# Norms whose two-input work leaves GpSimd, and a first ConvFFN pair that takes one token stream at a time

## The chip, the cores and the metric

The kernel runs on one core of one Trainium2 chip. The metric is the device time of one execution in microseconds (us). The engines are called TensorE (PE in the profile, its weight load PEld), VectorE (DVE), ScalarE (ACT), GpSimd (POOL) and SyncE (SP, which issues most transfers).

## The reference

One inference step of a decoder trunk of two layers over 544 tokens: 512 of a new sequence and 8 x 4 sampled ones. The model dimension is 1024, that of the ConvFFN 2816.

```python
for i in range(2):
    h = rms_norm(x, norm_mix[i])
    x = x + (conformer_conv(h) if i == 0 else stick_breaking_attention(h))
    h = rms_norm(x, norm_ffn[i])
    g = h @ w_gate[i]
    x = x + (silu(causal_dwconv(g)) * (h @ w_up[i])) @ w_down[i]
y = rms_norm(x, norm_final)
```

`rms_norm(x, g)` is `x * rsqrt(mean(x*x) + eps) * g` for each token, over the 1024 channels. The depthwise convolution of the ConvFFN (`causal_dwconv`) has a width of three tokens, so that a channel's gate is needed for all tokens before its taps. The outputs also hold the new rows of the convolution states and of keys and values.

## The kernel before, in words

**Layout.** `x` lies transposed in SBUF as `xT`: 128 partitions x 8 chunks `c` x 544 tokens. The tokens form two streams, SA (columns 0 to 255) and SB (the other 288, the sampled ones among them). A product of 128 output channels with one stream is a group of 24 matmuls into one PSUM bank. Each factor is split into a high and a low part, and a chunk takes three matmuls: `whi` by `XH`, `whi` by `XL`, `wlo` by `XH` (`gemm`, L425 to L427; in the ConvFFN `part`, L1251 to L1253; later quads L1439 to L1441).

**Weights.** A ring holds them: SyncE loads a `raw` slot, ScalarE copies it to `whi` (L325), VectorE subtracts for `wlo` (L328). Five slots are split ahead; when a slot is freed, the next is prepared.

**A norm** (class `Norm`, L489). When a chunk of `xT` has been evacuated (VectorE adds the PSUM bank to `x`: L1149, in the ConvFFN of layer 0 L1598), `feed` squares it on ScalarE (L516) and adds the square to the running sum `sqa` (L521). The add of the last chunk runs on VectorE, those of chunks 1 to 6 on GpSimd. The steps that follow are: `rstd` (a matmul with the matrix `mean_m` at L532, the root on ScalarE at L534, the reciprocal on VectorE at L535); then for each chunk the scaled `u = xT * rstd` (L539, for chunks 1, 2, 3, 5, 6 and 7 on GpSimd, `POOL_U`, and otherwise on VectorE), `XH` from `u` on ScalarE (L542) and `XL` from `u` and `XH` on VectorE (L545).

**Two ways of ordering.** Around the products of the mixers and the last downs the order is written by hand. `feed` issues its instructions in place, and the steps go into a queue `side`, of which `some` takes one at each quarter of a product. `take_due` puts a finished norm's steps into it: in `run_group` (L440) at quarter `DUE[last]` of a stream's first product, in `Wide` (L457) at quarter 3. In the ConvFFN and around the convolution a planner (class `Plan`, L75) orders the work: each operation comes with an engine, a cost and what it reads and writes, and the planner lays the operations out by these costs, with `urgent` as a bonus. The planned version of SB's norm ahead of a ConvFFN is `norm()` (L1272: matmul L1277, reciprocal L1282, `u` L1286, `XH` L1288, `XL` L1290); those of the convolution phase have their adds at L1092 and their `u` at L1123. Each engine executes its instructions in the order that results, so one that waits holds all behind it.

**The ConvFFN.** The hidden channels are taken in passes. The first pass begins with two pairs of channel groups by `gate_plain` (L1404) and `up` (L1496), called at L1573: gate 0 and gate 1 for SA, then both for SB, evacuated by ScalarE into `G`, then the taps of the width-three convolution (`taps`, VectorE L1393 and others), and then up 0 for SA and SB and up 1 for SA and SB; VectorE multiplies with the silu of the taps (L1504), and `low_h` splits the result into `HH` (ScalarE) and `HL` (VectorE, L1493). These products use the banks `tr` and `av` by turns (`psum2`, two of each); the tag `acc` has four. Pairs behind the first pass are taken as quads. After a pass come the downs of its channels and the transposes of the state rows (L1554).

**The final norm** (`Final.feed`) squares (L1637), adds chunks 1 to 6 on GpSimd (L1645) and transposes; L1680 to L1688 scale the rows.

Of the kernel before, what the change touches and what calls it, by code (L numbers as in the profile page):

```python
# [14 lines left out]
ALU = mybir.AluOpType  # L15
# [180 lines left out]
def tile_trunk(  # L196
# [260 lines left out]
    class Wide:  # L457


        def __init__(self, xh, xl, evac):  # L460
            self.xh, self.xl, self.evac = xh, xl, evac
# [27 lines left out]
    class Norm:  # L489
# [21 lines left out]
        def feed(self, st, c):  # L511
            c0, n = st
            if st is SA and c == 4:
                act_table("sqrt_and_others")
            sq = self.tile("sq", 3) if c else self.tile("sqa", 2)
            act.activation(sq[:, :n], xT[:, c, c0:c0 + n], AF.Square)  # L516
            if c == 0:
                self.acc[st] = sq
            else:
                a = self.acc[st][:, :n]  # L520
                (dve if c == NC - 1 else pool).tensor_tensor(a, sq[:, :n], a, op=ALU.add)  # L521
            if c == NC - 1:
                due.append(self.steps(st))

        def steps(self, st):
            c0, n = st
            cols = slice(c0, c0 + n)
            hold = {}

            def rstd():  # L530
                pt = bank("tr", uid("ms"))
                pe.matmul(pt[:, :n], mean_m, self.acc[st][:, :n], start=True, stop=True)  # L532
                hold["r"] = self.tile("rstd", 2)
                act.activation(hold["r"][:, :n], pt[:, :n], AF.Sqrt, bias=eps_t[:, 0:1], scale=1.0)  # L534
                dve.reciprocal(hold["r"][:, :n], hold["r"][:, :n])  # L535

            def scaled(c):
                u = hold[c] = self.tile("u", NC)
                (pool if c in POOL_U else dve).tensor_tensor(u[:, :n], xT[:, c, cols], hold["r"][:, :n], op=ALU.mult)  # L539

            def high(c):
                act.activation(XH[:, c, cols], hold[c][:, :n], AF.Copy, scale=pcol(self.row, c))  # L542

            def low(c):
                dve.scalar_tensor_tensor(XL[:, c, cols], hold[c][:, :n], pcol(self.row, c), XH[:, c, cols],  # L545
                                         op0=ALU.mult, op1=ALU.subtract)
# [86 lines left out]

    def psum(tag):
        return plan.tile(tag, banks[tag], lambda: bank(tag, uid(tag)))

    def on(eng, n, dve_cost, pool_cost):
        return (dve, "dve", 0.08 + n * dve_cost) if eng == "dve" else (pool, "pool", 0.1 + n * pool_cost)

    def product(slot, h):  # L640

# [439 lines left out]
    def normed(c, h):  # L1081

        c0, n = STREAMS[h]
        sq = plan.tile("sq" if c else "sqa", 2, lambda: nrm.tile("sq" if c else "sqa", 2))
        plan.op("act", 0.1 + n * 0.9e-3, lambda: act.activation(sq()[:, :n], xT[:, c, c0:c0 + n], AF.Square),
                r=[("x", c, h), "norm"], w=[sq])
        if c == 0:
            nrm.acc[h] = sq
            return
        a = nrm.acc[h]  # L1090
        e, name, cost = on("dve" if c == NC - 1 else "pool", n, 1.05e-3, 2.25e-3)
        plan.op(name, cost, lambda: e.tensor_tensor(a()[:, :n], sq()[:, :n], a()[:, :n], op=ALU.add), r=[sq], w=[a])  # L1092

    s0 = slot_no[0]
    slot_no[0] += NC
# [23 lines left out]
    plan.op("dve", 1.7, lambda: dve.reciprocal(rs()[:, :n], rs()[:, :n]), w=[rs])  # L1119
    for c in range(NC):  # L1120
        u = plan.tile("u", NC, lambda: nrm.tile("u", NC))
        e, name, cost = on("pool" if c in POOL_U else "dve", n, 1.05e-3, 2.25e-3)
        plan.op(name, cost, lambda c=c, u=u, e=e: e.tensor_tensor(u()[:, :n], xT[:, c, 0:n], rs()[:, :n], op=ALU.mult),  # L1123
                r=[rs, ("x", c, 0)], w=[u])
        plan.op("act", 0.32, lambda c=c, u=u: act.activation(XH[:, c, 0:n], u()[:, :n], AF.Copy,
                                                             scale=pcol(R_FFN, c)), r=[u], w=[("XH", c, 0)])
# [31 lines left out]
    def ffn(l, before, after):  # L1158
# [95 lines left out]

            return plan.op("pe", len(xs) * 3 * n * 0.4615e-3, f, w=[pt], r=[("slot", slot), *rd], follows=name)

        def group(slot, st, nk, xh, xl, keys):

            c0, n = st
            pt = psum2()  # L1260
# [11 lines left out]
        def norm():  # L1272
# [2 lines left out]
            pt, rs = psum("tr"), plan.tile("rstd", 2, lambda: before.tile("rstd", 2))  # L1275
            plan.op("in", ACC_LATE, lambda: None, w=["acc"])
            plan.op("pe", 0.55, lambda: pe.matmul(pt()[:, :n], mean_m, before.acc[SB][:, :n], start=True, stop=True),  # L1277
                    r=["acc"], w=[pt], urgent=2.0)
            plan.op("act", 0.36, lambda: act.activation(rs()[:, :n], pt()[:, :n], AF.Sqrt, bias=eps_t[:, 0:1], scale=1.0),
                    r=[pt, "table"], w=[rs])  # L1280
            plan.op("act", 1.3, lambda: act_table("silu_and_others"), w=["table"])
            plan.op("dve", 1.9, lambda: dve.reciprocal(rs()[:, :n], rs()[:, :n]), w=[rs])  # L1282
            for c in range(NC):
                u = plan.tile("u", NC, lambda: before.tile("u", NC))
                e, name, cost = (pool, "pool", 0.9) if c in POOL_U else (dve, "dve", 0.43)
                plan.op(name, cost, lambda c=c, u=u, e=e: e.tensor_tensor(u()[:, :n], xT[:, c, cols], rs()[:, :n], op=ALU.mult),  # L1286
                        r=[rs], w=[u])
                plan.op("act", 0.45, lambda c=c, u=u: act.activation(XH[:, c, cols], u()[:, :n], AF.Copy,  # L1288
                                                                   scale=pcol(before.row, c)), r=[u], w=[("X", c, 1, "h")])
                plan.op("dve", 0.5, lambda c=c, u=u: dve.scalar_tensor_tensor(  # L1290
                    XL[:, c, cols], u()[:, :n], pcol(before.row, c), XH[:, c, cols], op0=ALU.mult, op1=ALU.subtract),
                    r=[u, ("X", c, 1, "h")], w=[("X", c, 1), "normed"])

# [107 lines left out]
            plan.op("pool", 0.2, lambda: pool.tensor_copy(  # L1401
                SF[:, f, 2:18].rearrange("p (b t) -> p b t", b=NB), gs()[:, :, 4:6]), r=[g], w=[("SF", f)])

        def gate_plain(f2, s0):  # L1404
            gs = [G(f2 + i) for i in range(2)]
            for st in (SA, SB):
                for i in range(2):
                    pt = group(s0 + i, st, NC, XH, XL, xkeys)
                    c0, n = st
                    m, dst, new = places(gs[i], c0, n)  # L1410
                    plan.op("act", acost(m), lambda dst=dst, pt=pt, m=m: act.copy(dst(), pt()[:, :m]), r=[pt], a=[gs[i]])
                    if n > m:
                        plan.op("act", 0.2, lambda new=new, pt=pt, m=m, n=n: act.copy(new(), smp(pt(), m, n)), r=[pt], a=[gs[i]])
            for i in range(2):
                used(s0 + i)
                taps(f2 + i)

        def products(slots, tags, put):

# [73 lines left out]
            plan.op("dve", dcost(T), lambda: dve.tensor_tensor(  # L1493
                HL[:, f - k0, :], h(), HH[:, f - k0, :], op=ALU.subtract), r=[h], w=[("H", f - k0)])

        def up(f2, slots, k0):  # L1496
            for i in range(2):
                f = f2 + i
                h = buf(None, "h", [P, T], H_BUFS)
                s = sil[f]  # L1500
                for st in (SA, SB):
                    c0, n = st
                    pt = group(slots[i], st, NC, XH, XL, xkeys)
                    plan.op("dve", dcost(n), lambda c0=c0, n=n, pt=pt, h=h, s=s: dve.tensor_tensor(  # L1504
                        h()[:, c0:c0 + n], s()[:, c0:c0 + n], pt()[:, :n], op=ALU.mult), r=[pt, s], a=[h], urgent=U_POST)
                used(slots[i])
                low_h(f, k0, h)

        def up_quad(f2, slots, k0):
            hs = [buf(None, "h", [P, T], H_BUFS) for _ in range(2)]  # L1510

# [58 lines left out]
        s = first  # L1570
        (k0, nk), *rest = PASSES
        for f2 in range(k0, k0 + nk, 2):
            gate_plain(f2, s)  # L1573
            up(f2, (s + 2, s + 3), k0)
            s += 4

        for p0, pn in rest:
# [32 lines left out]
    class Final:  # L1610
# [17 lines left out]
        def feed(self, st, c):  # L1628
# [13 lines left out]
                                 for _ in self.blocks(st)]  # L1642
            elif c < NC - 1:
                a = self.acc[st][0][:, :n]
                pool.tensor_tensor(a, sq[:, :n], a, op=ALU.add)  # L1645

            def turn():
                if c % 4 == 0:
# [685 lines left out]
```

## Time and profile before

| | |
|---|---|
| time, median of 3 runs | 1355.88 us (1354.37 to 1357.83) |
| the profiled execution | 1356.08 us |
| its span in the trace | 1354.4 us |
| TensorE clock granted, mean | 0.992 |
| moved by DMA | 142.39 MB, 105 GB/s |
| GpSimd adds of squares L521 | 24, 23.3 us |
| GpSimd scaled chunks L539, L1286 | 18 and 12, 17.7 and 11.5 us |
| GpSimd work in the convolution phase L1092, L1123 | 12 and 6, 13.0 and 5.1 us |
| GpSimd adds of the final norm L1645 | 12, 9.2 us |

How to read the rows of the profile: a group of instructions shows line, engine, operation, out<-in by the program's names with partitions x elements, count | busy us, mean ns of one | idle time of the engine ahead of them, and what ended it. A row of the timeline shows its start in us from the span's start, how long it took (several instructions together where xN says so) and, in brackets, the engine's idle time before it and what ended that. A row of the waits shows the instruction that waited, what it waited for, and then the us in total, the times and the longest. A row of the windows shows the stretch, its length, and the busy time and the instructions of each engine in it. Matmuls overlap: their spacing, not their duration, says what one costs.

### The profile page before, as it was taken

What the parts mean: (1) busy time and instruction counts of PE and PEld (TensorE: products, weight loads), DVE (VectorE), ACT (ScalarE), POOL (GpSimd) and SP (SyncE); (2) the same over time, 40 slices, a digit from 0 to 9 for tenths busy, and PEclk for the clock granted to TensorE, in tenths of its full rate; (3) what the DMA queues carried; (4) which work ended last, traced back from release to release, by engine and by line L of the source; (5) the groups of instructions that cost most, each with busy time, mean ns of one, the idle gap of its engine ahead of it and who ended that gap; (6) DMA issues with size and microseconds to landing.
All of it is one profiled execution on the core that took longest, in us unless ns stands there. A gap on an engine that the chain in (4) does not pass through costs nothing.

```text
span 1354.4 us, 26784 instructions
## 1 busy us (share of the span) xinstructions
PE 1318.0 (97%) x11018; PEld 1242.8 (92%) x11018; DVE 975.6 (72%) x1650; ACT 668.9 (49%) x1242; POOL 240.5 (18%) x379
## 2 busy tenths in 40 slices
PE   8999999999999999998999999999899999999997
PEld 7897799899999999998999777769899999999997
DVE  5599785878987877856253776663897896786762
ACT  6421574545554554544333566753654654454452
POOL 3201014301010010033221242222520010000012
PEclk9899999999999999999999999999999999999998
DMA  8273523123233233235365242322122233233221
GB/s 227 67 185 103 126 95 109 32 86 102 87 111 101 73 111 114 76 118 181 126 205 166 80 129 90 102 94 63 63 79 83 92 110 110 75 100 109 86 73 66
DMA packets 124492, 142.39 MB, mean 105 GB/s; under 512 B 5672, under 2 KB 117992, under 8 KB 124099
## 3 DMA queue, kind: packets, MB, share of 16 engines
q1 hardware_dynamic: 118003, 122.43, 29.4%
q0 software_dynamic: 6080, 18.25, 4.3%
q8 instruction: 86, 1.41, 0.4%
q14 instruction: 35, 0.29, 0.1%
q10 hardware_dynamic: 288, 0.02, 0.0%
HBM read 129.34 MB, written 12.18 MB: 104 GB/s over the span
## 4 chain that ended last, share of the span: by engine, by line
PE 84%; DVE 9%; ACT 3%; issue 1%; DMA 1%; POOL 0%; SPq 0%; DVEq 0%; ACTq 0%; POOLq 0%
PE acc L1441 5%; PE acc L1439 5%; PE acc L1440 5%; PE acc L425 4%; PE acc L426 4%; PE acc L427 4%; PE tr L1252 4%; PE tr L1251 4%; PE tr L1253 3%; PE av L1251 3%; PE av L1252 3%; PE av L1253 3%; PE acc L651 3%; PE acc L653 3%; PE acc L652 3%; PE tr L1441 3%
## 5 line engine op out<-in xcount | busy, mean ns | idle before, releaser
L328 DVE TENSOR_TENSOR wlo<-raw,whi 128x1024 fp32r<-128x1024 f32 (+2 forms) x244 | 258.5, 1064 | 77.5 <-ACT whi L325 77.1
L325 ACT CAST whi<-raw 128x1024 fp32r<-128x1024 f32 (+2 forms) x244 | 223.0, 916 | 153.5 <-PE tr L1252 30.5
L651 PE MATMUL acc<-XH,whi 128*128 128x288 f32 (+1 forms) x384 | 114.9, 299 | 0.0
L653 PE MATMUL acc<-XH,wlo 128*128 128x288 f32 (+1 forms) x384 | 111.0, 289 | 1.8 <-DVE wlo L328 1.8
L652 PE MATMUL acc<-XL,whi 128*128 128x288 f32 (+1 forms) x384 | 111.3, 290 | 0.0
L425 PE MATMUL acc<-XH,whi 128*128 128x288 f32 (+1 forms) x360 | 107.8, 300 | 0.6 <-DVE xT L1598 0.6
L426 PE MATMUL acc<-XL,whi 128*128 128x288 f32 (+1 forms) x360 | 104.0, 289 | 0.0
L427 PE MATMUL acc<-XH,wlo 128*128 128x288 f32 (+1 forms) x360 | 103.6, 288 | 0.0
L1441 PE MATMUL acc<-TH,wlo 128*128 128x272 f32 x288 | 83.4, 290 | 0.0
L1439 PE MATMUL acc<-TH,whi 128*128 128x272 f32 x288 | 83.2, 289 | 0.0
L1440 PE MATMUL acc<-TL,whi 128*128 128x272 f32 x288 | 83.1, 288 | 0.0
L1475 ACT COPY G<-acc 128x272 f32<-128x272 f32 (+1 forms) x72 | 26.9, 373 | 110.3 <-PE acc L1441 95.4
L651 PEld LDWEIGHTS acc<-XH,whi 128*128 128x128 f32 x384 | 72.7, 189 | 2.7 <-issue 2.1
L653 PEld LDWEIGHTS acc<-XH,wlo 128*128 128x128 f32 x384 | 72.8, 190 | 2.2 <-DVE wlo L328 2.2
L1252 PE MATMUL av<-HL,whi 128*128 128x288 f32 (+1 forms) x256 | 74.4, 290 | 0.0
L1251 PE MATMUL av<-HH,whi 128*128 128x288 f32 (+1 forms) x256 | 74.3, 290 | 0.0
L1253 PE MATMUL av<-HH,wlo 128*128 128x288 f32 (+1 forms) x256 | 74.0, 289 | 0.0
L1251 PE MATMUL tr<-HH,whi 128*128 128x256 f32 (+1 forms) x256 | 73.6, 288 | 0.0
L1252 PE MATMUL tr<-HL,whi 128*128 128x256 f32 (+1 forms) x256 | 73.4, 287 | 0.0
L652 PEld LDWEIGHTS acc<-XL,whi 128*128 128x128 f32 x384 | 72.8, 190 | 0.5
L1253 PE MATMUL tr<-HH,wlo 128*128 128x256 f32 (+1 forms) x256 | 73.0, 285 | 0.0
L1393 DVE SCALAR_TENSOR_TENSOR cv<-G,fprm,cv 128x560 f32<-128x560 f32 x88 | 69.9, 798 | 4.2 <-ACT cv L1390 3.0
(461 smaller groups left out, 4456.0 us busy)
## 6 DMA issues: line engine op xcount, KB each, us to landing
raw<-in_ffn_w_gate_dram SPq DMA_DIRECT2D x22, 1024.0 KB
raw<-in_ffn_w_up_dram SPq DMA_DIRECT2D x22, 1024.0 KB
raw<-in_ffn_w_down_dram SPq DMA_DIRECT2D x24, 768.0 KB
raw<-in_attn_w_qkv_dram SPq DMA_DIRECT2D x12, 1024.0 KB
raw<-in_conv_w_in_dram SPq DMA_DIRECT2D x6, 1024.0 KB
rep<-glu SPq DMA_DIRECT2D x36, 142.0 KB
raw<-in_conv_w_out_dram SPq DMA_DIRECT2D x4, 1024.0 KB
raw<-in_ffn_w_down_dram SPq DMA_DIRECT2D x8, 512.0 KB
```

What stands on the lines that cost most here:

```text
L325: act.copy(hi[:, :n, :], src)
L328: dve.tensor_tensor(lo[:, :n, :], src, hi[:, :n, :], op=ALU.subtract)
L425: pe.matmul(o, hi[:, k, :], xh[:, k, c0:c0 + n], start=(k == 0), stop=False)
L426: pe.matmul(o, hi[:, k, :], xl[:, k, c0:c0 + n], start=False, stop=False)
L427: pe.matmul(o, lo[:, k, :], xh[:, k, c0:c0 + n], start=False, stop=(k == nk - 1))
L651: pe.matmul(o, hi[:, k, :], XH[:, k, c0:c0 + n], start=(k == 0), stop=False)
L652: pe.matmul(o, hi[:, k, :], XL[:, k, c0:c0 + n], start=False, stop=False)
L653: pe.matmul(o, lo[:, k, :], XH[:, k, c0:c0 + n], start=False, stop=(k == NC - 1))
L1251: pe.matmul(o, hi[:, j + k, :], xh, start=(start and k == 0), stop=False, **kw)
L1252: pe.matmul(o, hi[:, j + k, :], xl, start=False, stop=False, **kw)
L1253: pe.matmul(o, lo[:, j + k, :], xh, start=False, stop=(stop and k == len(xs) - 1), **kw)
L1441: pe.matmul(o, lo[:, j + k, :], xh, start=False, stop=(k == 3), **kw)
```

## The change

Four things are edited. (1) Every add of squares and every scaled chunk `u` is on VectorE: in `feed`, `scaled`, the convolution phase, `norm()` and `Final.feed`; `POOL_U` and the helper `on` go. In the hand-ordered norm, `first` now scales two chunks, and each later step one more. (2) The places at which `take_due` stands: `DUE` becomes (3,2), and `Wide` takes it in its second product, by default at quarter 0. (3) In the planned `norm()` the matmul loses `urgent=2.0`, and costs are set anew. (4) `plain_pair` replaces `gate_plain` and `up` in the first pass: for each stream gate 0, gate 1, up 0, up 1; the ups go to `acc` banks; the taps and the multiplications follow after both streams. The planner then lays out this work anew.

```diff
-DUE = (3,0)
-POOL_U = (1, 2, 3, 5, 6, 7)
+DUE = (3,2)
...
-                if i == 0:
-                    places[3] = [take_due, some]
+                if i == 1:
+                    places[self.due] = [take_due, some]
...
-                (dve if c == NC - 1 else pool).tensor_tensor(a, sq[:, :n], a, op=ALU.add)
+                dve.tensor_tensor(a, sq[:, :n], a, op=ALU.add)
...
-                (pool if c in POOL_U else dve).tensor_tensor(u[:, :n], xT[:, c, cols], hold["r"][:, :n], op=ALU.mult)
+                dve.tensor_tensor(u[:, :n], xT[:, c, cols], hold["r"][:, :n], op=ALU.mult)
...
-                for c in range(NC):
-                    if c == 0 or c in POOL_U:
-                        scaled(c)
+                for c in range(2):
+                    scaled(c)
...
-                    if c + 2 < NC and c + 2 not in POOL_U:
+                    if c + 2 < NC:
...
-                    r=["acc"], w=[pt], urgent=2.0)
+                    r=["acc"], w=[pt])
...
-            plan.op("dve", 1.9, lambda: dve.reciprocal(rs()[:, :n], rs()[:, :n]), w=[rs])
+            plan.op("dve", 1.8, lambda: dve.reciprocal(rs()[:, :n], rs()[:, :n]), w=[rs])
...
-        def gate_plain(f2, s0):
+        def plain_pair(f2, s0, k0):
+
             gs = [G(f2 + i) for i in range(2)]
+            ups = {}
             for st in (SA, SB):
+                c0, n = st
                 for i in range(2):
                     pt = group(s0 + i, st, NC, XH, XL, xkeys)
...
+                for i in range(2):
+                    ups[i, st] = group(s0 + 2 + i, st, NC, XH, XL, xkeys, "acc")
             for i in range(2):
                 used(s0 + i)
                 taps(f2 + i)
+            for i in range(2):
+                used(s0 + 2 + i)
+                f = f2 + i
+                h = buf(None, "h", [P, T], H_BUFS)
+                for c0, n in (SA, SB):
+                    plan.op("dve", dcost(n), lambda c0=c0, n=n, pt=ups[i, (c0, n)], h=h, s=sil[f]: dve.tensor_tensor(
+                        h()[:, c0:c0 + n], s()[:, c0:c0 + n], pt()[:, :n], op=ALU.mult), r=[ups[i, (c0, n)], sil[f]], a=[h],
+                        urgent=U_POST)
+                low_h(f, k0, h)
...
-                pool.tensor_tensor(a, sq[:, :n], a, op=ALU.add)
+                dve.tensor_tensor(a, sq[:, :n], a, op=ALU.add)
```

More of the change, by code (lines that the diff above doesn't have):

```diff
@@ L457, in tile_trunk, with __init__ @@
     class Wide:
-        def __init__(self, xh, xl, evac):
-            self.xh, self.xl, self.evac = xh, xl, evac
+        def __init__(self, xh, xl, evac, due=0):
+            self.xh, self.xl, self.evac, self.due = xh, xl, evac, due
             self.s0 = slot_no[0]
@@ L1090, in normed @@
         a = nrm.acc[h]
-        e, name, cost = on("dve" if c == NC - 1 else "pool", n, 1.05e-3, 2.25e-3)
-        plan.op(name, cost, lambda: e.tensor_tensor(a()[:, :n], sq()[:, :n], a()[:, :n], op=ALU.add), r=[sq], w=[a])
+        plan.op("dve", 0.08 + n * 1.05e-3, lambda: dve.tensor_tensor(a()[:, :n], sq()[:, :n], a()[:, :n], op=ALU.add), r=[sq], w=[a])
     s0 = slot_no[0]
@@ L1121, in tile_trunk @@
         u = plan.tile("u", NC, lambda: nrm.tile("u", NC))
-        e, name, cost = on("pool" if c in POOL_U else "dve", n, 1.05e-3, 2.25e-3)
-        plan.op(name, cost, lambda c=c, u=u, e=e: e.tensor_tensor(u()[:, :n], xT[:, c, 0:n], rs()[:, :n], op=ALU.mult),
+        plan.op("dve", 0.08 + n * 1.05e-3, lambda c=c, u=u: dve.tensor_tensor(u()[:, :n], xT[:, c, 0:n], rs()[:, :n], op=ALU.mult),
                 r=[rs, ("x", c, 0)], w=[u])
@@ L1255, in part, with group @@
             return plan.op("pe", len(xs) * 3 * n * 0.4615e-3, f, w=[pt], r=[("slot", slot), *rd], follows=name)
-        def group(slot, st, nk, xh, xl, keys):
+        def group(slot, st, nk, xh, xl, keys, tag=None):
             c0, n = st
-            pt = psum2()
+            pt = psum(tag) if tag else psum2()
             last = None
@@ L1281, in norm @@
             plan.op("act", 1.3, lambda: act_table("silu_and_others"), w=["table"])
-            plan.op("dve", 1.9, lambda: dve.reciprocal(rs()[:, :n], rs()[:, :n]), w=[rs])
+            plan.op("dve", 1.8, lambda: dve.reciprocal(rs()[:, :n], rs()[:, :n]), w=[rs])
             for c in range(NC):
                 u = plan.tile("u", NC, lambda: before.tile("u", NC))
-                e, name, cost = (pool, "pool", 0.9) if c in POOL_U else (dve, "dve", 0.43)
-                plan.op(name, cost, lambda c=c, u=u, e=e: e.tensor_tensor(u()[:, :n], xT[:, c, cols], rs()[:, :n], op=ALU.mult),
+                plan.op("dve", dcost(n), lambda c=c, u=u: dve.tensor_tensor(u()[:, :n], xT[:, c, cols], rs()[:, :n], op=ALU.mult),
                         r=[rs], w=[u])
@@ L1494, in low_h @@
                 HL[:, f - k0, :], h(), HH[:, f - k0, :], op=ALU.subtract), r=[h], w=[("H", f - k0)])
[L1496 to L1507, printed above, removed]
         def up_quad(f2, slots, k0):
@@ L1572, in ffn @@
         for f2 in range(k0, k0 + nk, 2):
-            gate_plain(f2, s)
-            up(f2, (s + 2, s + 3), k0)
+            plain_pair(f2, s, k0)
             s += 4
```

5 lines of the change are left out of this document (1 added, 4 removed).

## The prediction, made before the changed kernel was run

> **What bounds the kernel now.** I read the page first: the busy time of each engine, then the chain of work that ended last.
>
> ```profile
> PE 1318.0 (97%) x11018; PEld 1242.8 (92%) x11018; DVE 975.6 (72%) x1650; ACT 668.9 (49%) x1242; POOL 240.5 (18%) x379
> ...
> PE 84%; DVE 9%; ACT 3%; issue 1%; DMA 1%; POOL 0%; SPq 0%; DVEq 0%; ACTq 0%; POOLq 0%
> ```
>
> TensorE is busy for 97% of the span and holds 84% of the chain. The change adds and removes no matmul, so all it can win is TensorE's idle time, some 36 us, and only the part that norms and first pairs cause. The view of TensorE's waits names those; `sqa` is a norm's sum of squares, `XH` and `XL` its output.
>
> ```profile
> PE ms L532 <- DVE sqa L521: 3.6, 2, 2.9
> ...
> PE av L1252 <- DVE XL L1290: 2.0, 4, 0.7
> ...
> PE av L1251 <- ACT XH L1288: 1.8, 2, 0.9
> PE acc L425 <- DVE xT L1598: 1.8, 2, 1.2
> ...
> PE tr L1277 <- DVE sqa L521: 1.5, 1, 1.5
> ...
> PE tr L1252 <- DVE XL L1290: 1.1, 1, 1.1
> ```
>
> They come to 11.8 us in twelve waits. The view by windows says in which stage they lie, and how full VectorE is there.
>
> ```profile
> core 0: us, PE busy (x) PEld busy (x) DVE busy (x) ACT busy (x) POOL busy (x), PEclk, DMA share, GB/s
> 230.00:245.00 15.00, 11.90 (x92) 10.80 (x92) 10.02 (x16) 7.41 (x15) 6.05 (x8) 1.00 0.08 32
> 245.00:285.00 40.00, 40.00 (x320) 39.93 (x319) 35.44 (x57) 21.68 (x42) 8.08 (x12) 1.00 0.19 56
> 285.00:305.00 20.00, 20.00 (x160) 20.00 (x159) 13.54 (x24) 6.44 (x12) 1.16 (x2) 1.00 0.29 95
> 591.00:622.00 31.00, 26.34 (x196) 25.46 (x195) 19.88 (x28) 13.94 (x26) 10.68 (x12) 1.00 0.37 135
> 940.00:972.00 32.00, 27.76 (x193) 26.16 (x192) 25.48 (x36) 16.86 (x31) 16.34 (x18) 0.95 0.21 66
> ```
>
> TensorE idles 3.1 us in the first pair of layer 0 (230 to 245), 4.7 in the norm ahead of attention (591 to 622), 4.2 in layer 1's FFN norm and first pair (940 to 972). From 245 to 285 it never idles, and there VectorE is 89% full.
>
> **Durations.** All two-input norm work of GpSimd goes to VectorE; a group and the timelines of both engines in the norm ahead of attention give the price on both.
>
> ```profile
> L521 POOL TENSOR_TENSOR sqa<-sq,sqa 128x288 f32<-128x288 f32 x12 | 13.7, 1141 | 23.3 <-ACT sq L516 23.2
> ```
> ```profile
> 596.23 5.76 POOL L539 TENSOR_TENSOR u<-xT,rstd 128x256 f32<-128x256 f32 x6 [5.46 <-DVE rstd L535]
> ```
> ```profile
> 597.92 1.70 DVE L328 TENSOR_TENSOR wlo<-raw,whi 128x1024 fp32r<-128x1024 f32 x1 [0.67 <-ACT whi L325]
> 599.54 1.85 DVE L545 SCALAR_TENSOR_TENSOR XL<-u,prm,XH 128x256 fp32r<-128x256 f32 x2
> ...
> 602.20 0.41 DVE L539 TENSOR_TENSOR u<-xT,rstd 128x256 f32<-128x256 f32 x1
> 603.27 1.22 DVE L328 TENSOR_TENSOR wlo<-raw,whi 128x1024 fp32r<-128x1024 f32 x1 [0.66 <-ACT whi L325]
> 604.41 0.87 DVE L545 SCALAR_TENSOR_TENSOR XL<-u,prm,XH 128x256 fp32r<-128x256 f32 x2
> ```
>
> A scaled chunk `u` of 256 columns costs 5.76 / 6 = 0.96 us on GpSimd and 0.41 on VectorE. While GpSimd scales (596.2 to 602.0), VectorE's own work is slower: two `XL` take 1.85 us instead of 0.87, a `wlo` 1.70 instead of 1.22. So six `u` moved onto VectorE cost it 6 x 0.41 = 2.5 us and give back up to 8 x 0.49 = 3.9 on the eight `XL`: in a stage where GpSimd scales, the move is about free for VectorE, and the chunks come sooner. The adds (1.14 us on GpSimd, about 0.4 on VectorE by the row of `u`) are different: an add waits for its square on ScalarE, and all that stands behind it on VectorE waits too.
>
> **Layer 0, first pair.** Here all products of stream SA (four of 24 matmuls) go first, so that SB's norm has 48 matmuls more of cover.
>
> ```profile
> 230.82 0.38 PE L1251 MATMUL av<-XH,whi 128*128 128x256 f32 x1
> ...
> 233.76 0.65 PE L1277 MATMUL tr<-sqa,mean_m 128*128 128x288 f32 x2
> ...
> 238.13 0.40 PE L1251 MATMUL av<-XH,whi 128*128 128x288 f32 x1 [0.90 <-ACT XH L1288]
> ...
> 283.64 0.60 PE L1554 MATMUL av<-ident,SF 128*18 128x128 f32 x4
> ```
>
> The wait of 0.90 at 238.13 is the first of several. The window of 245 to 285, where nothing stalls, gives 40.00 / 320 = 0.125 us for a matmul, both streams mixed. The 384 matmuls of both pairs need 384 x 0.125 = 48.0 us, the mean matmul ahead of SB 0.6 (L1277). From 230.82 that ends at 279.4; before, 283.64: 4.2 us to win. In the built order the mean matmul follows up 0 of SA (about 236.5), then gate 1 and up 1 of SA keep TensorE to 242.7, and by a layout of VectorE's queue SB's `XL` 0 is there at 240.9 and `XL` 7 at 245.8, each ahead of its use. So these stalls go. What is late next is VectorE: its 35.4 us of work of 245 to 285 is the same and has 4.2 us less time.
>
> ```profile
> 284.18 0.72 DVE L1493 TENSOR_TENSOR HL<-h,HH 128x544 fp32r<-128x544 f32 x1
> ...
> 285.95 0.72 DVE L1493 TENSOR_TENSOR HL<-h,HH 128x544 fp32r<-128x544 f32 x1
> ```
>
> The last two `HL` of the pass must stand when the first quad's downs reach them. Laid out from 245.75, VectorE has 36.7 us of work to them and ends at about 283.0 and 283.65, and TensorE, 4.2 us sooner, asks for the first at 282.4: a stall of 0.6, and 0.2 more at the following quad. I take +3.4 (2.5 to 4.2). After 285 VectorE has 32% of its time free (13.54 of 20), so nothing more is carried on.
>
> [...]
>
> **Norm ahead of attention (591 to 622).** The norm's steps are taken one per quarter of a product, at places written by hand. The rstd step now stands nine matmuls later in SB's stream, and every add of c = 1 to 6 stands on VectorE behind its evacuation.
>
> ```profile
> 609.61 0.40 PE L425 MATMUL acc<-HH,whi 128*128 128x288 f32 x1 [1.24 <-DVE xT L1598]
> ...
> 612.81 0.35 PE L425 MATMUL acc<-XH,whi 128*128 128x256 f32 x1 [0.55 <-DVE xT L1598]
> ...
> 618.74 0.72 PE L532 MATMUL ms<-sqa,mean_m 128*128 128x288 f32 x2 [2.87 <-DVE sqa L521]
> ```
> ```profile
> 616.45 1.66 POOL L521 TENSOR_TENSOR sqa<-sq,sqa 128x288 f32<-128x288 f32 x2 [2.29 <-ACT sq L516]
> ```
>
> Before, the wait of 2.87 ends with two GpSimd adds of 0.83 in a row and VectorE's of 0.46. On VectorE the three take some 1.2 instead of 2.1, but the rstd step ends about 2.1 us later than before, and each add holds VectorE for about 0.66 (its evacuation, then the square). By my layout the wait for the last evacuations is 1.65 and 0.95 (1.24 and 0.55 before), the one at L532 falls to 2.4, and the second product of q behind it starts a little sooner. Sum: +0.5, with -1 and +2 as ends, since the cover of the adds (VectorE idle in waits for `whi`, 0.66 at 597.92 and 603.27) is partly used twice.
>
> **Layer 1.** The same two parts meet: the last products of the attention output run while SA is normed.
>
> ```profile
> 944.35 0.70 PE L532 MATMUL ms<-sqa,mean_m 128*128 128x256 f32 x2 [0.76 <-DVE sqa L521]
> ...
> 965.82 0.40 PE L1251 MATMUL av<-XH,whi 128*128 128x288 f32 x1 [0.90 <-ACT XH L1288]
> ...
> 1011.78 0.49 PE L1554 MATMUL av<-ident,SF 128*18 128x128 f32 x3
> ```
> ```profile
> 956.89 1.43 DVE L545 SCALAR_TENSOR_TENSOR XL<-u,prm,XH 128x256 fp32r<-128x256 f32 x2
> 958.24 0.45 DVE L1149 TENSOR_TENSOR xT<-acc,xT 128x288 f32<-128x288 f32 x1
> ```
> ```profile
> 958.78 0.45 ACT L516 ACTIVATE sq<-xT 128x288 f32<-128x288 f32 x1 [1.06 <-DVE xT L1149]
> ```
> ```profile
> L325 ACT CAST whi<-raw 128x1024 fp32r<-128x1024 f32 (+2 forms) x244 | 223.0, 916 | 153.5 <-PE tr L1252 30.5
> ```
>
> The 0.76 goes, since rstd is taken two steps later. But in the built order SA's `XL` 6, a `wlo` and `XL` 7 now stand behind the evacuation that ends at 958.7 and its add. From 958.7 on, hand-over 0.1, square 0.45, add 0.4, `XL` 0.43, `wlo` 1.2 and `XL` 0.43 give 961.7 at the soonest. In the built order a weight copy (0.92 us, L325) stands ahead of the square on ScalarE: 962.6, and with three or four more hand-overs of 0.1, 963.0; before, `XL` 7 ended at 958.3 (956.89 + 1.43). I take 963.0: the first gate's last chunk holds TensorE to 963.3, a new stall of about 4.3 us. After it come 15 products, 360 matmuls x 0.125 = 45.0 us, and the mean matmul's 0.6, without a stall: 1008.9, where before the pass ended at 1011.8. That is +2.9, less 0.9 for the same late `HL` as in layer 0: +2.0 (1 to 3).
>
> **Final norm.** Its adds move to VectorE too; the one of c = 6 now stands ahead of the last evacuation.
>
> ```profile
> 1343.97 0.42 DVE L1149 TENSOR_TENSOR xT<-acc,xT 128x256 f32<-128x256 f32 x1 [2.02 <-PE acc L427]
> ```
> ```profile
> 1342.46 1.54 POOL L1645 TENSOR_TENSOR sq<-sq,sq 128x256 f32<-128x256 f32 x2 [2.53 <-ACT sq L1637]
> ```
>
> That evacuation is due at 1343.97; behind two squares and two adds it starts at 1344.56: -0.6 (-1.2 to 0), right on the tail. **The conv norms** (L1092, L1123) cost nothing: they lie beside the conv weight products, VectorE has room there, and the first bank that waits for it is due 0.5 us after its evacuation in my layout; without that cover it is up to -1.
>
> **Sum.** 3.4 + 0.5 + 2.0 - 0.6 = 5.3 us off the profiled execution (1356.08; its span 1354.4 and 1.7 around it), which gives 1350.8; the median of the runs, 1355.88, lies 0.2 lower, so I say 1350.6. The ends of the parts, with the conv norms' -1, are a gain of 0.3 and one of 9.2: 1346.7 to 1355.6.
>
> **The rivals.** (1) *VectorE becomes the bound of the first pass.* For it: 89% full from 245 to 285, and now the tap chains of four gate groups start at the same time as before while the downs come sooner. Then the pass ends when `HL` did before, and 3.4 and 2.0 are gone: 0.5 - 0.6 is left, 1356. Against it: the 4.2 us that VectorE lacks were free before (40.00 - 35.44 = 4.6). (2) *No wait takes the place of the old ones.* The three windows' idle time of 3.1 + 4.7 + 4.2 = 12.0 goes whole: 1344. Against it: the `XL` 7 of layer 1 and the later rstd. (3) *The adds make VectorE late in SB's streams*, the case on the other side. If each of the twelve adds of SB (six ahead of attention, six in layer 1) waits for a square that stands behind one more weight copy on ScalarE (0.92 us, L325), 12 x 0.92 = 11.0 us are lost on the path: 5.3 - 11.0 is 5.7 slower, 1361.6. It decides from the point where ScalarE has no gap ahead of the square; against it, ScalarE is 45% busy in 591 to 622 (13.94 of 31). That the change does not do what it says is excluded by the built order: SA's ups stand between gates, and no norm add is left on GpSimd.
>
> **How the numbers follow.** Forecast 0.51, rival 1 0.26, rival 2 0.09, rival 3 0.14. The measurement tells 0.3%, 4.1 us, from no change: bounds 1351.8 and 1359.9. Of the forecast 0.41 lies below 1351.8 and 0.10 within; rival 2 is faster; rival 1 is within but for 0.02; rival 3 is slower: 0.50, 0.34, 0.16. Forecast, rival 1 and nearly half of rival 2 hold 0.80: 1345 to 1359.
>
> **What would show it.** First pairs: no wait of L1251 or L1252 for SB's `XL` in layer 0, the transposes of L1554 at about 279.4 instead of 283.64, and a wait for `HL` L1493 below 1 us; over 3 us is rival 1. Layer 1: one wait of about 4 us for `XL` L545 in the first gate, none later; 8 us or more is rival 3. Ahead of attention: L532 waiting 2 to 3 us. `XL` of 256 columns near 440 ns. The forecast is wrong if VectorE idles much longer than 0.7 us ahead of the adds, or if SB's mean matmul is issued late and its `XL` still holds TensorE.

## The result, and the profile after

The changed kernel takes 1358.29 us (median of 18 runs, 1353.98 to 1361.88), the kernel before 1355.83 (18 runs, 1353.88 to 1357.83): a ratio of 1.0020, 95% interval 1.0010 to 1.0029. It is 0.2% slower, where 0.4% faster was forecast. The profiled execution is one of its fastest (1354.24 us, span 1352.5, mean granted clock 0.993); one of 1360.19 us ran at 0.988. The line numbers of the changed kernel are shifted: L1244 to L1246 are L1251 to L1253 of before, L773 is L778, L531 is L532, L544 is L545, L1128 is L1135, L1546 is L1554.

The page first, with the rows that were shown of before:

```profile
PE 1318.2 (97%) x11018; PEld 1243.3 (92%) x11018; DVE 989.0 (73%) x1734; ACT 668.7 (49%) x1242; POOL 158.2 (12%) x295
...
PE 85%; DVE 8%; ACT 3%; DMA 2%; issue 1%; POOL 0%; SPq 0%; DVEq 0%; ACTq 0%; POOLq 0%
```

GpSimd has lost 82 us of busy time and VectorE has gained 13, though 84 instructions moved. TensorE's share has not changed; 2% of the chain is now DMA, where it was 1%. The waits of TensorE say where:

```profile
PE av L773 <- DMA rep<-glu: 5.2, 2, 3.8
PE av L1245 <- DVE XL L544: 3.0, 3, 1.7
PE ms L531 <- DVE sqa L520: 2.2, 1, 2.2
...
PE acc L424 <- DVE xT L1589: 2.0, 2, 1.4
...
PE ms L1661 <- DVE sq L1636: 0.4, 1, 0.4
PE av L1246 <- DVE wlo L327: 0.4, 1, 0.4
PE av L1245 <- DVE HL L1498: 0.3, 2, 0.2
```

The waits of the planned norms for SB's `XL` and `XH` are gone. In their place stands a wait for a transfer in the convolution phase, `rep<-glu`, which no step of the prediction touched, and one of 3.0 us for `XL` L544 (SA in layer 1), which it had. The windows of the three stages, and of the stretch behind layer 1's first gate:

```profile
228.50:243.50 15.00, 14.86 (x127) 14.47 (x126) 5.65 (x12) 5.37 (x11) 0.33 (x2) 1.00 0.00 1
243.50:281.00 37.50, 37.50 (x296) 37.50 (x295) 35.85 (x61) 22.43 (x46) 5.78 (x12) 1.00 0.18 58
594.00:620.00 26.00, 21.77 (x163) 20.91 (x162) 20.52 (x37) 12.69 (x24) 0.00 (x0) 1.00 0.33 113
936.00:968.00 32.00, 28.91 (x199) 27.87 (x198) 18.22 (x36) 12.11 (x22) 0.00 (x0) 0.89 0.21 66
954.00:960.00 6.00, 2.91 (x19) 2.09 (x17) 5.25 (x11) 3.42 (x6) 0.00 (x0) 0.93 0.12 39
960.00:966.00 6.00, 6.00 (x27) 5.96 (x28) 1.84 (x5) 0.79 (x2) 0.00 (x0) 0.50 0.54 175
966.00:970.00 4.00, 4.00 (x34) 3.88 (x33) 2.92 (x4) 2.25 (x4) 0.00 (x0) 1.00 0.00 0
```

Layer 0's first pair no longer stalls (14.86 of 15 us busy). The last three rows are what to look at. From 954 to 960 TensorE is busy for 2.91 of 6 us; then it is busy throughout, but at a granted clock of 0.50, and does 27 matmuls in 6 us where 48 would fit at 0.125. From 966 the clock is 1.00 again; the trace's record of the clock has it at 0.50 for 6.8 us, from 959.2 on.

Now the convolution phase. GpSimd's timeline, after and before:

```profile
127.91 1.91 POOL L759 TENSOR_TENSOR wdg<-eye,tapc 128x1024 f32<-128x1024 f32 x1 [4.72 <-PE av L773]
129.77 0.62 POOL L1128 DMA_DIRECT2D out_dram<-in_state_conv_dram  x1
232.26 0.33 POOL L1362 COPY G<-fprm 128x16 f32<-128x16 f32 x2 [101.87 <-ACT fprm L1073]
```
```profile
227.74 0.80 POOL L1092 TENSOR_TENSOR sqa<-sq,sqa 128x288 f32<-128x288 f32 x1 [1.27 <-ACT sq L1085]
228.49 0.61 POOL L1135 DMA_DIRECT2D out_dram<-in_state_conv_dram  x1
```

Line L1128 is `pool.dma_start(out=sc_s[0, :, 0:PAST - NI, :], in_=state_conv[0, :, NI:PAST, :])`: 832 KB of state rows, copied to the output. It waits for nothing but its place in GpSimd's queue. Before, eighteen adds and scaled chunks of the convolution phase stood ahead of it; now none of them does, and it goes out 99 us sooner. SyncE's timeline at that time, after and before, and TensorE's wait after:

```profile
130.13 3.70 SPq L742 DMA_DIRECT2D glu<-ext_p  x3
137.24 5.54 SPq L746 DMA_DIRECT2D rep<-glu  x12
```
```profile
132.34 1.32 SPq L747 DMA_DIRECT2D glu<-ext_p  x3
134.17 6.85 SPq L751 DMA_DIRECT2D rep<-glu  x12
```
```profile
141.91 1.93 PE L773 MATMUL av<-rep,wdg 128*32 128x256 f32 x32 [3.81 <-DMA rep<-glu]
```

The three stores of `glu` take 3.70 us to issue instead of 1.32, and the loads of `rep`, which read them back, begin 7.1 us behind the first store instead of 1.8. TensorE waits 3.8 us for them. Of the three stores it is the last that is long (2.84 us instead of 0.46); by what the copy holds it back, no run shows.

### The profile page after: what moved, and what is told of

The parts are those of the page before. It is cut to its first block, busy times and chain, and to the rows that moved or that the text cites. A ratio compares the mean times of both kernels' runs of the same rounds, so it can differ in the third digit from the quotient of the medians.

```text
span 1352.5 us, 26751 instructions
## 1 busy us (share of the span) xinstructions
PE 1318.2 (97%) x11018; PEld 1243.3 (92%) x11018; DVE 989.0 (73%) x1734; ACT 668.7 (49%) x1242; POOL 158.2 (12%) x295
## 4 chain that ended last, share of the span: by engine, by line
PE 85%; DVE 8%; ACT 3%; DMA 2%; issue 1%; POOL 0%; SPq 0%; DVEq 0%; ACTq 0%; POOLq 0%
PE acc L1446 5%; PE acc L1444 5%; PE acc L1445 5%; PE acc L424 4%; PE acc L425 4%; PE acc L426 4%; PE acc L646 3%; PE acc L648 3%; PE acc L647 3%; PE av L1245 3%; PE tr L1244 3%; PE av L1246 3%; PE tr L1245 3%; PE av L1244 3%; PE tr L1246 3%; PE tr L1446 3%
## 5 line engine op out<-in xcount | busy, mean ns | idle before, releaser
L646 PEld LDWEIGHTS acc<-XH,whi 128*128 128x128 f32 x384 | 72.7, 189 | 2.7 <-issue 2.1
L1246 PE MATMUL av<-HH,wlo 128*128 128x288 f32 (+1 forms) x256 | 74.1, 290 | 0.4 <-DVE wlo L327 0.4
L1244 PE MATMUL av<-HH,whi 128*128 128x288 f32 (+1 forms) x256 | 74.4, 290 | 0.0
L1244 PE MATMUL tr<-HH,whi 128*128 128x256 f32 (+1 forms) x256 | 73.4, 287 | 0.0
L1246 PE MATMUL tr<-HH,wlo 128*128 128x256 f32 (+1 forms) x256 | 73.0, 285 | 0.0
L424 PEld LDWEIGHTS acc<-XH,whi 128*128 128x128 f32 x360 | 67.7, 188 | 3.4 <-issue 3.1
```

The source lines that it names most:

```text
L424: pe.matmul(o, hi[:, k, :], xh[:, k, c0:c0 + n], start=(k == 0), stop=False)
L646: pe.matmul(o, hi[:, k, :], XH[:, k, c0:c0 + n], start=(k == 0), stop=False)
L1244: pe.matmul(o, hi[:, j + k, :], xh, start=(start and k == 0), stop=False, **kw)
L1246: pe.matmul(o, lo[:, j + k, :], xh, start=False, stop=(stop and k == len(xs) - 1), **kw)
```

## The experiments

The theory after the first look had two parts. **Q:** the copy that GpSimd's queue no longer holds back delays the convolution phase. **C:** a stretch in which TensorE does little is followed by some microseconds of half clock, so that a stall of 4 us in one piece costs more than the same stall in pieces. The rivals: the time is lost in VectorE's queue (D), and the transfer wait belongs to one execution alone. All ratios are to the kernel before, run on the same chip in the same rounds.

| experiment | median us | ratio (95%) |
|---|---|---|
| e1 changed kernel again | 1359.32 | 1.0033 (1.0018 to 1.0047) |
| e2 before again | 1353.88 | 1.0004 (0.9994 to 1.0015) |
| e3 norms only | 1358.29 | 1.0027 (1.0014 to 1.0040) |
| e4 pair only | 1347.09 | 0.9953 (0.9940 to 0.9966) |
| e5 copy moved | 1353.34 | 0.9992 (0.9981 to 1.0002) |
| e6 before, conv norms on VectorE | 1360.22 | 1.0041 (1.0026 to 1.0056) |
| e7 e5 and layer 1's stall filled | 1351.82 | 0.9979 (0.9967 to 0.9991) |
| e8 changed, adds on GpSimd | 1345.46 | 0.9922 (0.9907 to 0.9936) |
| e9 e5 with DUE (3,0) | 1350.58 | 0.9969 (0.9959 to 0.9978) |
| e10 e8 with DUE (3,0) | 1343.35 | 0.9926 (0.9913 to 0.9940) |
| e11 changed, one add on GpSimd | 1351.62 | 0.9977 (0.9967 to 0.9986) |
| e12 e11 with DUE (3,0) | 1348.76 | 0.9948 (0.9933 to 0.9964) |

**Both kernels again (e1, e2).** No edit.

> The changed kernel once more, for a second profile. In the first one TensorE stands still for 4 us in layer 1's first gate (954.5 to 958.8 us) and its granted clock is 0.50 from 959 to 966. Theory C (clock): that stretch and the half clock behind it come back in this profile, and the runs spread as before, 1354 to 1362 us, time and mean granted clock going together by 1.35 us for each 0.001 of clock. Rival W (transfer): the waits of TensorE for the transfers rep<-glu in the convolution phase (5.2 us in the first profile, none in that of the kernel before) are part of the change and come back too, at 4 to 5 us. By theory C alone they do not.

> The kernel before once more, for a second profile. Theory C: its stalls in layer 1 are spread out (0.8, 1.5, 0.9, 0.7, 0.3 us), so that half clock behind them is short (0.60 and 0.55 in 968 to 972) and its runs lie close, 1354 to 1358 us with a granted clock of 0.990 to 0.993. Rival D (VectorE is the new bound and the clock plays no part) expects no connection of time and clock in either kernel. A ratio of 0.998 to 1.002.

The wait for `rep<-glu` is back in e1 (5.4 us in two) and absent in e2. In e1 it also has a half clock behind it, which the first profile did not; TensorE's timeline and the windows of e1:

```profile
143.45 3.17 PE L773 MATMUL av<-rep,wdg 128*32 128x256 f32 x25 [3.77 <-DMA rep<-glu]
```
```profile
142.00:148.00 6.00, 4.55 (x44) 2.48 (x48) 1.87 (x5) 0.00 (x0) 0.00 (x0) 0.50 0.99 202
...
964.00:970.00 6.00, 5.07 (x24) 4.87 (x25) 3.47 (x7) 1.22 (x3) 0.00 (x0) 0.56 0.55 175
```

So one and the same wait of 3.8 us was followed by full clock in one execution and by 6.8 us at 0.50 in the other. Between two fixed matmuls around it (numbers 1240 and 1320 of the trace, in order of time) lie 6.3 us in the kernel before and in e2, 10.0 in the first profile of the changed kernel and 12.6 in e1.

The traces' record of the clock shows where it was at 0.50. In the first profile of the changed kernel that is from 37.60 us for 3.413 us, from 959.20 for 6.827 and from 1344.90 to the end of the program; in the first profile of the kernel before, from 36.57 for 6.827, from 883.07 and from 968.41 for 3.413 each, and from 1347.29 to the end. In both, the starts lie whole multiples of 3.413 us from the first one (270 and 383 times in the one, 248, 273 and 384 times in the other). Taken in steps of that length which keep to an execution's own starts, the wait looks like this, in the windows of the first profile and then of e1:

```profile
136.58:139.99 3.41, 1.51 (x29) 0.65 (x20) 3.25 (x10) 0.47 (x1) 0.00 (x0) 1.00 0.65 178
139.99:143.41 3.42, 1.50 (x28) 1.13 (x32) 2.23 (x7) 0.00 (x0) 0.00 (x0) 1.00 1.08 217
```
```profile
138.66:142.07 3.41, 1.02 (x20) 0.37 (x12) 3.17 (x10) 0.47 (x1) 0.00 (x0) 1.00 0.69 179
142.08:148.90 6.82, 5.45 (x52) 2.94 (x56) 1.82 (x4) 0.00 (x0) 0.00 (x0) 0.50 0.86 175
```

In the first profile the wait is shared by two steps, with 1.51 and 1.50 us of matmuls, and the clock stays at 1.00; in e1 most of it falls into one, with 1.02, and the next 6.82 us run at 0.50. Of the two others with the same wait, e3 has 1.00 us in the step and half clock behind it, e6 1.39 and 1.76 and none. What decides it, the runs do not show. The busy time of a step does not tell it: the clock was at 0.50 also behind 1.42 us (955.79 to 959.20 in the first profile) and, in the first profile of the kernel before, behind 1.62 (965.00 to 968.41) and 2.14 (879.66 to 883.07).

Over the 18 first runs of the changed kernel the time falls by 1.1 us for each 0.001 of mean granted clock (1.35 was expected), with a correlation of -0.94; in e2's twelve runs the tie is weak (-0.33). Most of the changed kernel's spread is the clock's. The rest shows in the traces as the start: for its first 500 matmuls one execution takes 72.9 us and another 78.8, over all profiles.

**Each half of the change alone (e3, e4).** e3 keeps `gate_plain` and `up`, e4 the old norms.

```diff
-            plain_pair(f2, s, k0)
+            gate_plain(f2, s)
+            up(f2, (s + 2, s + 3), k0)
```

> The norms, DUE, Wide's place and the planner's costs as changed, the first pair in the old order. Theory C: the 4 us stretch of layer 1 comes from the norm (XL 6 and 7 of SA behind an evacuation and its add), so it stays, with half clock behind it, and the pair's gain of 3 to 4 us in layer 0 goes in part: 1358 to 1363 us. Rival D: the pair is what makes VectorE late, so without it the kernel is at or under the time before, 1352 to 1356.

> The first pair as changed, the norms as before with GpSimd's adds and scaled chunks. Theory C: SA's XL 7 of layer 1 is ready at 958.3 again, no stretch of 4 us, and the pair's cover takes the stalls of SB in both layers: 4 us in layer 0 less 1.4 given back by late HL, 3 to 4 in layer 1: 1348 to 1352. Rival D: VectorE, slowed by GpSimd beside it, gives the gain back behind the first pair: 1354 to 1358.

The pair is worth 0.5% by itself, somewhat more than expected; rival D falls. The norms cost 0.3%, and bring the wait for `rep<-glu` with them (5.1 us in e3, none in e4). The two do not add up: their product is 0.9980, and both together are at 1.0020, and at 1.0033 in e1, which ran in the same rounds. The traces show where the pair's gain went. For the stretch of layer 1's norm and first pass (matmuls 7700 to 8500) the kernel before takes 108.7 us, e4 104.0, e3 109.7 and the changed kernel 109.0: the pair alone wins 4.7 us there, and with the changed norms nothing of it is left. In layer 0 (2104 to 2700) it keeps its gain: 79.1 before, 76.1 in e4, 76.5 in the changed kernel.

**The copy (e5, e6, e11).** e5 takes the copy out of its place and puts it behind the first ConvFFN. e6 is the kernel before with its conv adds and scaled chunks on VectorE, e11 the changed kernel with one of those adds back on GpSimd. The diffs of e5 and of e11:

```diff
-    pool.dma_start(out=sc_s[0, :, 0:PAST - NI, :], in_=state_conv[0, :, NI:PAST, :])
...
+        if l == 0:
+            pool.dma_start(out=sc_s[0, :, 0:PAST - NI, :], in_=state_conv[0, :, NI:PAST, :])
```
```diff
-        plan.op("dve", 0.08 + n * 1.05e-3, lambda: dve.tensor_tensor(a()[:, :n], sq()[:, :n], a()[:, :n], op=ALU.add), r=[sq], w=[a])
+        e, name, cost = (pool, "pool", 0.1 + n * 2.25e-3) if h and c == NC - 2 else (dve, "dve", 0.08 + n * 1.05e-3)
+        plan.op(name, cost, lambda: e.tensor_tensor(a()[:, :n], sq()[:, :n], a()[:, :n], op=ALU.add), r=[sq], w=[a])
```

> The changed kernel, with the one copy of the convolution state (state_conv to the output, 832 KB, L1128, issued from GpSimd's queue) taken out of its place and issued behind the first ConvFFN. Theory Q (queue): with the norm adds gone from GpSimd nothing holds that copy back, so it goes out at 130 us instead of 228, and its packets stand ahead of the stores of glu and the loads of rep for which TensorE waits; that costs 4 us, and 2.6 us of half clock behind it where the wait is long. So here: no wait for rep<-glu, and 4 to 6 us less than the changed kernel, 1352 to 1355. If the copy has no part in it (only layer 1's stall and clock): as the changed kernel, 1358 to 1359.

> The kernel before, with only the adds and scaled chunks of the convolution phase (L1092, L1123) moved from GpSimd to VectorE. Theory Q: these 18 instructions were all that held the copy of the convolution state back, so it goes out near 130 us and TensorE waits 4 to 6 us for rep<-glu, half clock behind it included: 1358 to 1361. As the prediction had it (the move costs nothing): 1353 to 1355.

> The changed kernel with one single add on GpSimd again: that of chunk 6 of SB in the convolution phase (L1087), which stands ahead of the copy of the convolution state in GpSimd's queue. In e5 the copy was placed behind the ConvFFN in the text, but went out at 14.0 us, and so may have cost something at the start. Theory Q: one add is enough to hold the copy back to about 228 us; no wait for rep<-glu, nothing at the start: 4 to 6.3 us less than the changed kernel, 1350 to 1354, and the stall and half clock of layer 1 unchanged. If the copy has no part in it: 1358 to 1359.

In e6 GpSimd and TensorE show the same picture as in the changed kernel:

```profile
131.24 0.62 POOL L1133 DMA_DIRECT2D out_dram<-in_state_conv_dram  x1
```
```profile
143.24 3.01 PE L778 MATMUL av<-rep,wdg 128*32 128x256 f32 x52 [3.67 <-DMA rep<-glu]
```

In e11 one add of 0.80 us holds the copy to its old place:

```profile
224.99 0.80 POOL L1087 TENSOR_TENSOR sqa<-sq,sqa 128x288 f32<-128x288 f32 x1 [95.74 <-ACT sq L1080]
225.73 0.61 POOL L1129 DMA_DIRECT2D out_dram<-in_state_conv_dram  x1
```

The move of the conv norms alone, which the prediction priced at nothing, costs 0.41% (5.6 us by the medians; the profile has 3.6 of it between matmuls 1240 and 1320, with no half clock), and one add given back takes the changed kernel from 1.0020 to 0.9977, some 6 us. In e11 a wait of 1.8 us for `rep<-glu` is still listed, but it costs nothing: between matmuls 1240 and 1320 lie 6.3 us as before. Theory Q holds. e5 did not do quite what it was meant to: nothing holds its copy either, and it went out at 14.0 us.

```profile
L1583 POOL DMA_DIRECT2D out_dram<-in_state_conv_dram x1: 577/577/577, 14.0 to 14.0; - x1
```

That is clear of the convolution, but it lies among the first loads; e5 is 0.15% above e11, and e9 0.21% above e12, on different chips and with intervals that overlap. The early transfer is the likely reason: the three profiles with it (e5, e7, e9) take 78.1 to 78.8 us for their first 500 matmuls, the eleven others 72.9 to 76.8. No run tried it by itself.

**The half clock (e7).** Useless matmuls fill the stall of layer 1's first gate in e5.

```diff
+FILL = 32
...
+                    if l == 1 and slot == first and start and k == 0 and n == SA[1]:
+                        for _ in range(FILL):
+                            pe.matmul(o, hi[:, 0, :], xh, start=True, stop=True, **kw)
```

> As e5_late_copy, with 32 useless matmuls of 256 columns ahead of the first matmul of layer 1's first gate (their sums are written over). They take 32 x 0.117 = 3.7 us of the 4 us for which TensorE would stand still there. Theory C (clock): the stretch no longer empties TensorE, its granted clock stays at 1.00 behind it, and the 2.5 to 3.5 us that half clock cost from 959 to 966 are gone: 1349 to 1352. Rival: the clock falls for another reason or costs nothing; then the time is that of e5_late_copy or some tenths more.

The windows behind the first gate, first of e5, then of e7, and e7's extra matmuls:

```profile
960.00:966.00 6.00, 5.48 (x25) 5.19 (x26) 3.26 (x7) 0.99 (x3) 0.00 (x0) 0.50 0.54 175
```
```profile
958.00:964.00 6.00, 5.96 (x48) 5.65 (x48) 4.09 (x9) 1.74 (x4) 0.00 (x0) 1.00 0.50 170
964.00:970.00 6.00, 6.00 (x53) 6.00 (x52) 5.39 (x10) 4.38 (x8) 0.00 (x0) 1.00 0.03 8
```
```profile
953.51 4.00 PE L1246 MATMUL av<-XH,whi 128*128 128x256 f32 x32
```

The pass has 32 matmuls more to do and is shorter: from the first matmul of the gate to the first transpose of L1546 it takes 55.6 us in the changed kernel, 55.2 in e5, 52.9 in e7. The clock stays at 1.00 throughout. So the half clock costs 2.3 to 2.7 us here, and the stall some 3.5 us more (e7's 52.9 against 49.4 in e12, which has no stall), which the filling cannot give back. The median of the runs moved by 1.5 us, less than the 2.5 to 3.5 expected, and the intervals of e5 and e7 overlap: what carries the reading is the clock of the profile, which the filling kept at 1.00.

**What makes SA's `XL` late in layer 1 (e8, e9, e10, e12).** e8 puts the adds of squares back on GpSimd and leaves the scaled chunks on VectorE; the other three set `DUE = (3,0)` in e5, e8 and e11.

```diff
-                dve.tensor_tensor(a, sq[:, :n], a, op=ALU.add)
+                (dve if c == NC - 1 else pool).tensor_tensor(a, sq[:, :n], a, op=ALU.add)
...
-DUE = (3,2)
+DUE = (3,0)
```

> The changed kernel with the adds of squares back on GpSimd (feed, the convolution phase, the final norm); the scaled chunks stay on VectorE. Theory Q: the copy of the convolution state waits behind GpSimd's adds again, no wait for rep<-glu. If the adds are also what makes SA's XL 6 and 7 late in layer 1 (VectorE held by each add's square), that stall falls from 4 to under 2 us and no half clock follows: 1346 to 1350. If the later place of the rstd step does it alone, the stall stays at 3 to 4 us: 1350 to 1354.

> As e5_late_copy (the changed kernel with the copy of the convolution state moved), with DUE = (3,0) as in the kernel before: the steps of SA's norm in layer 1 are taken two quarters of a product sooner. Theory P (place): the later place is a good part of the 4 us for which the first gate waits for XL 6 and 7; two quarters are 12 matmuls, 1.6 us, so the stall falls to about 2.5 us, half clock becomes rarer, and rstd's matmul waits 0.8 us as before: 1351 to 1353.5. Theory A (adds alone): the adds hold VectorE wherever the steps stand; the stall stays at 3.5 to 4 us and the time is that of e5_late_copy, 1353 to 1354.

> As e8_adds_pool (the changed kernel with the adds of squares on GpSimd), with DUE = (3,0). There the first gate of layer 1 still waited 1.3 us for XL, and TensorE's clock fell to 0.63 behind it for a short while. Theory P: with the steps two quarters sooner that wait goes, and so does the half clock, for 0.8 us at rstd's matmul: 1343 to 1345, under e8's 1345.5. Theory A: without adds on VectorE the place of the steps no longer matters, and the 0.8 us at rstd make it 1345.5 to 1346.5.

> As e11_one_add, with DUE = (3,0). In e9 the two edits together took away the stall of layer 1's first gate and left 0.7 and 0.4 us of waits at the mean matmuls. So 3 to 5 us under e11: 1346 to 1349; under e9 (1350.6) by what the copy at 14 us cost there. If it is above e9, the early copy cost nothing and the 228 us place does.

TensorE's waits from 935 on in e8, e9 and e10, in this order:

```profile
PE av L1246 <- DVE XL L544: 1.1, 1, 1.1
PE av L1245 <- ACT XH L541: 0.2, 1, 0.2
```
```profile
PE ms L531 <- DVE sqa L520: 0.7, 1, 0.7
PE tr L1269 <- DVE sqa L520: 0.4, 1, 0.4
```
```profile
PE ms L531 <- DVE sqa L520: 0.8, 1, 0.8
```

Either edit takes most of the stall away: without adds on VectorE it is 1.3 us, with the steps two quarters sooner it is gone, at 0.7 to 0.8 us for `rstd`. The pass that took 55.5 us in e11 takes 49.4 in e12, 52.3 in e8 and 48.8 in e10. So theory P is right in e9 and e12, and more so than expected; the adds by themselves were not the cause, but adds and late place together. e10 and e8 are the same by their ratios (0.9926 and 0.9922, intervals that overlap), though the pass in e10 is 3.5 us shorter: e10's median is 2.1 us under e8's, but it ran on another chip, where the kernel before was 0.9 us faster too. Both have the lowest ratios of all, 0.7 to 0.8% under the kernel before. e8 is also 0.3% under e4 on the same chip, with intervals that do not overlap; it differs from e4 by the scaled chunks on VectorE, the later places of the steps and the planner's costs. The intervals of e10 and e12 overlap a little. In the norm ahead of attention (matmuls 5000 to 5200) e8 and e10 take 29.0 us, the changed kernel 30.3 and the kernel before 30.7.

## Why the prediction was wrong

- **First pair of layer 0: right.** 4.3 us won by the middle of the pair (between matmuls 2104 and 2176 the changed kernel takes 4.3 us less), and 4.0 at its end: the transposes stand at 281.09 after a start at 232.26, which is 48.8 us, against 52.8 before and 48.6 forecast. Given back behind that are 0.7 us at 285 for the late `HL`, as forecast (0.8), and another 0.7 at 302.6 for a late `wlo`, which was not. That leaves 2.7 us of the 3.4 forecast.

```profile
232.26 0.38 PE L1244 MATMUL av<-XH,whi 128*128 128x256 f32 x1
...
281.09 0.60 PE L1546 MATMUL av<-ident,SF 128*18 128x128 f32 x4
284.98 0.40 PE L1245 MATMUL av<-HL,whi 128*128 128x288 f32 x1 [0.16 <-DVE HL L1498]
302.61 0.40 PE L1246 MATMUL av<-HH,wlo 128*128 128x288 f32 x1 [0.40 <-DVE wlo L327]
```

- **Norm ahead of attention: right in the first profile** (0.4 won, 0.5 forecast; L531 waits 2.24 where 2.4 was laid out). In e1 and e12 this wait too has a half clock behind it (0.50 for 3.4 us), and the stage loses 1.1 to 1.2 against the first profile of the kernel before instead. That is not the change's doing: e4 and e6, whose norm here is the old one, have it as well and lose 1.5 to 1.8.
- **Final norm: right,** 0.4 lost and 0.6 forecast.
- **The conv norms "cost nothing": this step failed.** The adds and scaled chunks themselves are free on VectorE, as forecast: from matmul 1320 to 1960 the kernel before takes 66.3 us, the changed kernel 66.3 and e11 66.4. But the step looked at the engine that takes the work and not at the queue that loses it. In GpSimd's queue they were what held an 832 KB copy back. Between matmuls 1240 and 1320 that costs 3.7 us, and 6.3 where half clock follows.
- **Layer 1: the stall was right and its price was not.** SA's last `XL` held the first gate, by three waits that make 3.0 us of idle time; from matmul to matmul TensorE loses 4.1 us there against the kernel before, and 4.3 were forecast:

```profile
955.34 0.39 PE L1245 MATMUL av<-XL,whi 128*128 128x256 f32 x1 [0.38 <-DVE XL L544]
958.38 0.39 PE L1245 MATMUL av<-XL,whi 128*128 128x256 f32 x1 [1.69 <-DVE XL L544]
959.91 0.58 PE L1245 MATMUL av<-XL,whi 128*128 128x256 f32 x1 [0.90 <-DVE XL L544]
```

  "After it come 15 products, 360 matmuls x 0.125" is the step that failed: the next 6.8 us ran at 0.50, for which the sum had no term. The pass takes 55.6 us where 52.0 was forecast (956.9 to 1008.9) and 54.9 was taken before; e7, with the stall filled, takes 52.9. The kernel before had a half clock there as well in its first profile (0.95 on average in 940 to 972, by the row in the prediction; none in e2); the working shows that column. With the earlier `rstd`, which wins 1.0 us, and the late `HL` behind the pass, which costs 0.6 (0.9 forecast), layer 1 loses 0.3 where 2.0 was to be won.

The sum of the profile's own parts then is 2.7 + 0.4 - 0.3 - 0.4 = 2.4 us won, less 3.7 to 6.3 for the transfer: 1.3 to 3.9 lost, where the medians differ by 2.5. The two profiled executions differ the other way (1352.5 against 1354.4) by things that the change does not touch: 2.2 us in the first 500 matmuls, and 0.9 behind a half clock at 883.1 (0.50 for 3.413 us) that only the profile of the kernel before has of these two. Of the rivals none was the case. That the time lies in the range is luck: its upper end was there for rival 1, no gain at all. The sign was wrong, and rival 3, the one on the other side, named another mechanism: the adds' waits, which were already in the forecast.

## What to carry to other kernels

When work leaves an engine, read what stands behind it in that engine's queue, its transfers above all: the copy here waited for nothing but its turn, went out at 129.77 us instead of 228.49 when the work ahead of it was gone, and met the one transfer that the bound engine waited for (3.8 us). A stall of the bound engine has a length and a shape: some 4 us in several stalls and in one piece were not the same here. The piece in layer 1 has 6.8 us at 0.50 behind it in all five traces that have it (the first profile, e1, e3, e5, e11); the spread stalls of the kernel before had 3.4 us in its first profile and none in e2. Look for the granted clock in short windows right behind each stall. Of two operations on the slower engine (a scaled chunk takes 0.96 us on GpSimd and 0.41 on VectorE) the one to move is that whose input is ready long before: here the versions with the scaled chunks on VectorE and the adds, which wait for a square, on GpSimd are the fastest (1343.35 us in e10, 1345.46 in e8). That it is the wait that makes the adds dear was argued, not tried by itself.

## What the runs showed of the hardware

With a copy of 832 KB within DRAM issued from GpSimd's queue at 129.77 us instead of 228.49, three stores on SyncE's queue took 3.70 us to issue instead of 1.32, and the loads of what they store began 7.1 us behind the first store instead of 1.8; with the copy back at 225.73 (e11) TensorE took 6.3 us between matmuls 1240 and 1320 instead of 10.0. The granted clock fell to 0.50, in the first profiles of both kernels for 3.413 or 6.827 us at a time and once more at the end of the program. It fell behind 3.41 us with 1.02 (e1), 1.42 (first profile), 1.62 and 2.14 us (kernel before) of matmuls, and not behind two such steps with 1.51 and 1.50 (first profile). The same wait of 3.8 us had it in one execution and not in another; by what, no run shows. Over the 18 first runs of the changed kernel, which spread by 0.6%, time and mean granted clock have a correlation of -0.94. VectorE's work was slower beside GpSimd's (two `XL` 1.85 us instead of 0.87 in the kernel before), but that alone does not say where work belongs: the best versions (e8, e10) leave the adds on GpSimd, and move only the scaled chunks.
